# Attention's softmax sums applied at the output projection's loads, and the last input chunks in another order

## The chip, the cores and the metric

The kernel runs on one core of a Trainium2 chip. The metric is the device time of the whole kernel in microseconds (us); lower is better. Five engines work side by side, each strictly in the order of its own instructions: TensorE (PE, matrix products and transposes), VectorE (DVE), ScalarE (ACT, activations and copies), GpSimd (POOL) and SyncE (SP), which here only issues DMA transfers. An instruction that waits holds up everything behind it on its engine.

## The reference

One encoder layer over a 1024 x 1024 activation: an input projection feeds two head groups side by side, 8 attention heads (64 wide, 2 key/value heads) and 4 heads of a bidirectional mLSTM; an output projection and a SwiGLU feed-forward follow. What the change touches is the softmax of the attention and the projection that reads it:

```python
def one_block(q_blk):
    s = jnp.einsum('bkgqd,bksd->bkgqs', q_blk, kt).astype(jnp.float32) * scale
    p = jax.nn.softmax(s, axis=-1).astype(vt.dtype)
    return jnp.einsum('bkgqs,bksd->bkgqd', p, vt)
...
    mix = jnp.concatenate([y_attn, y_mem], axis=-1) @ w_out[l]
    x = x + g1[:, None, :] * mix
```

Softmax divides each row of exponentials by its sum. The division is by a number of that query row alone, so it may be done on the probabilities or, later, on the attention's output.

## The kernel before

Nearly every product is made of three matmuls on a high and a low part of each operand (`mm3`, lines 322 to 325), so every operand tile is split: ACT copies it into the high part, then DVE or POOL subtracts that from the original to get the low part.

The program is written out by a planner. `Clock` (line 131) keeps estimated times of the engines and a heap of steps; `ck.chain(delay, steps...)` runs steps one after another when their flags are set; `ck.streams(mains, fills)` writes PE's work: whichever main stream is ready goes first, and a fill stream goes when none is. The estimates only set the order in which instructions stand; on the chip each engine follows that order and waits on semaphores. Where this text says that something "stands" somewhere, it speaks of that order.

The stages: the head of the kernel (adaLN, the first projections, up to about 150 us of the profile), attention (about 153 to 484 us), mLSTM with the output projection (to about 680 us), the feed-forward (the rest).

**Attention.** There are 64 steps q, 8 heads times 8 blocks of 128 query rows (`NQ`, `NJ`). `scores` computes a 128 x 1024 score tile in PSUM (`S`), DVE takes its row maximum (`top`), ACT makes the exponentials into the tile `P` with their row sum (`exp`), DVE takes the reciprocal of the sum, POOL multiplies the whole tile `P` by it (`norm`). Only then is the flag `Pok[q]` set, on which `turned` waits: it transposes `P` on PE in two halves into PSUM tiles `T`, ACT and DVE split them into `PT`. `values` multiplies `PT` with the values into `av`, and each pair of steps stores 64 x 256 outputs, `avt`, to the DRAM tile `ya_d`. `colq` (line 308) is a 128 x 8 x 8 tile that holds the scale factor of each query row and head, read as the scale of `exp` and in `top`. `att_q(h)` loads and splits the queries of head h into `qs`.

**Fills in attention.** The rest of the input projection runs in the gaps, in the order of the list `IN` (line 49): "q" units are queries, "f" units (`conv_unit`) make 512-column products, copied out of PSUM as `xp` and then run through a five-tap convolution on DVE (`y`), "t" units (`chunk_unit`) make eight 256-column chunks each, copied out as `vstg` and stored to `v_d` or `o_d`. In attention the fills have one PSUM bank ("acc" and "acct" with one buffer between them): a next unit can start only when ACT has copied the last one out. Besides, `ada_late` streams 64 tiles of the adaLN weights through POOL (a multiplication, `ada`) and ACT (their sum).

**The output projection.** `load_y` (line 1274) loads four 128 x 512 tiles `yat` for each half of the columns and each of the two head groups (`ya_d` for attention, `ym_d` for mLSTM) and splits them into `yah` on ACT and `yal` on POOL. The first call of it, for attention's first half, is made while the last chunk unit ("t", 3) runs beside the start of mLSTM. `mq` are the query tiles of mLSTM, loaded one ahead, `wv` its weighted values on POOL. All loads and stores named here are issued by SP, through the helper `dma`.

Of the kernel before, what the change touches and what calls it, by code (L numbers as in the profile page):

```python
# [11 lines left out]
F32 = mybir.dt.float32  # L12
F32R = mybir.dt.float32r
BF16 = mybir.dt.bfloat16
AF = mybir.ActivationFunctionType
OP = mybir.AluOpType
# [4 lines left out]
P = 128  # L21
S = 1024
D = 1024
KT = D // P
HALF = 512
NH = 2
NJ = S // P
EPS = 1e-6
QK = 0.25 * 128 ** -0.5
AH = 8  # L30
DH = 64
# [15 lines left out]
AHEAD = 2  # L47
NP = NF // 2
IN = [("q", 2), ("q", 3), ("f", 0), ("f", 4), ("t", 2), ("f", 1),
      ("f", 5), ("f", 2), ("t", 1), ("f", 6), ("f", 3), ("f", 7), ("t", 3)]  # L50
MIX = [("o", i) for i in range(16)] + [("m", (i + 8) % 16) for i in range(16)]
FF = [("b", p) for p in range(NB)] + [("v", 0)] + [("s", (p, i)) for p in range(1, NP - 1) for i in range(2)] + [("v", NP - 1)]
SET = ["A11", "A12", "S2", "S3", "S1", "A22", "S4"]
# [207 lines left out]
def layer_kernel(ctx, tc, xT, c, w_ada, vecs, cons, rope, w_f, w_fT, w_t0, w_t, w_o, w_gu, w_d, out):  # L261
# [39 lines left out]
    mqk_d = [dram.tile([P, S], F32, name=f"mqk_d{i}") for i in range(8)]  # L301
    v_d = [dram.tile([P, NJ, 2, P], F32, name=f"v_d{i}") for i in range(2)]
    o_d = [dram.tile([P, NJ, 2, P], F32, name=f"o_d{i}") for i in range(2)]
    ya_d = [dram.tile([P, S], F32, name=f"ya_d{i}") for i in range(4)]
    x1_d = [dram.tile([P, S], F32, name=f"x1_d{i}") for i in range(KT)]
    act_d = [{m: dram.tile([P, HALF], F32, name=f"act_d{p}{m}") for m in DOWN} for p in range(NP)]
# [25 lines left out]
    def halves(n):  # L332
        return slice(n * HALF, (n + 1) * HALF)
# [42 lines left out]
    with tc.manual_schedule():  # L376
# [801 lines left out]
        def att_q(h):  # L1178
            if h:
                qd = ap.tile([P, S], F32, tag="qd", name="qd", bufs=1)  # L1180
                src = q_d[h // 2][(h % 2) * DH:(h % 2 + 1) * DH]
                dma(qd[0:DH], src)
                there = ck.chain(dma(qd[DH:P], src), lambda: None)
            else:
                qd, there = q0_at
            qs = ap.tile([P, S], F32R, tag="qs", name="qs")
            Q[h] = qs, ck.chain(0.0, there, lambda: act.activation(qs, qd, AF.Copy),
                                lambda: (gps if h else dve).tensor_sub(qs[DH:P], qd[DH:P], qs[DH:P].bitcast(F32)))

        def scores():  # L1190

            for q in range(NQ):
# [18 lines left out]

                def exp(st=st, sp=sp, cq=cq, q=q, f=f):
                    Pt[q] = ap.tile([P, S], F32, tag="P", name="P", bufs=3)
                    act.activation(Pt[q], sp, AF.Exp, bias=st[:, 1:2], scale=cq, accum_out=st[:, 2:3])
                    f.set(ck, ck.fin + LAT)

                def norm(st=st, q=q):
                    gps.tensor_scalar(Pt[q], Pt[q], st[:, 3:4], 0.0, op0=OP.mult, op1=OP.add)

                ck.chain(LAT, top, exp, lambda st=st: dve.reciprocal(st[:, 3:4], st[:, 2:3]), norm, flag=Pok[q])  # L1220

        def turned():

# [50 lines left out]
        def load_y(mem, n):  # L1274
# [6 lines left out]
            for k in range(4):  # L1281
                if mem and k == MH - 1:
                    Y[mem, n].append(y_last[n])
                    continue
                e = [None, None, Flag()]
                Y[mem, n].append(e)

                def load(e=e, k=k):
                    t = op.tile([P, HALF], F32, tag="yat", name="yat", bufs=4)
                    arrive = dma(t, (ym_d if mem else ya_d)[k][:, halves(n)])  # L1290

                    def hi():
                        e[0] = op.tile([P, HALF], F32R, tag="yah", name="yah", bufs=yb)
                        act.activation(e[0], t, AF.Copy)

                    def lo():
                        e[1] = op.tile([P, HALF], F32R, tag="yal", name="yal", bufs=yb)
                        gps.tensor_sub(e[1], t, e[0].bitcast(F32))

                    ck.chain(arrive, *used, hi, lo, flag=e[2])  # L1300

                ck.chain((2.0 if mem else 0.0) + (2.5 * k if at else 0.0), *([ym_ok[k][n]] if mem else []), load)

# [1089 lines left out]
```

## Time and profile before

| what | us |
|---|---|
| median of 3 runs (lowest, highest) | 1325.05 (1324.91, 1332.57) |
| the profiled execution's own time | 1328.24 |
| its span, first to last instruction | 1326.4 |
| PE busy (share of the span) | 1268.8 (96%) |
| DVE busy | 1044.1 (79%) |
| ACT busy | 705.8 (53%) |
| POOL busy | 524.5 (40%) |

The page of the profile lists each engine's busy time, the span in 40 slices, the chain of work that ended last, and groups of instructions. Group lines read: source line, engine, operation, output<-input, shape, count | busy us, mean ns of one | idle time just before them, and what ended most of it. L102 is the line of the helper that records all DVE, ACT and POOL operations, so there the tile's name tells them apart. In a timeline the first two columns are the start and the duration in us, and brackets give the idle time before an instruction and who ended it. PEclk is the share of its full clock that PE was granted.

### The profile page before, as it was taken

How to read it: one execution, taken by the hardware profiler on the slowest of the kernel's cores; microseconds unless marked ns; L12 is line 12 of the kernel's file. 1: busy time of each engine (PE TensorE's matmuls, PEld its weight loads, DVE VectorE, ACT ScalarE, POOL GpSimd, SP SyncE). 2: the span in 40 equal slices, each digit the busy share in tenths (PEclk: the TensorE clock that was granted, in tenths of full speed). 3: DMA queues.
4: the chain of work that ended last, by engine and by line, in shares of the span. 5: the costliest groups of instructions: out<-in, count | busy, mean ns of one | idle time of the engine just before them, and what ended most of it. 6: DMA issues, size and time to landing. Idle time of an engine off the chain costs nothing.

```text
span 1326.4 us, 19735 instructions
## 1 busy us (share of the span) xinstructions
PE 1268.8 (96%) x6656; PEld 1071.9 (81%) x6656; DVE 1044.1 (79%) x1679; ACT 705.8 (53%) x1349; POOL 524.5 (40%) x455
## 2 busy tenths in 40 slices
PE   9999789999899999999999999999999998999997
PEld 7887678878887888787877888888888886888886
DVE  7958798879578956898789988866676755788886
ACT  6583667877587746555686332233332334454453
POOL 0072467766476515532153355544555420000002
PEclk9999899999999999999999999999999999999999
DMA  9547423333233237633552443323333259733324
GB/s 375 196 151 196 127 99 121 96 94 106 81 120 94 64 117 259 202 100 124 191 184 71 159 135 128 112 104 115 109 104 110 88 192 335 274 100 93 94 60 163
DMA packets 104469, 187.04 MB, mean 141 GB/s; under 512 B 11568, under 2 KB 33200, under 8 KB 104368
## 3 DMA queue, kind: packets, MB, share of 16 engines
q1 hardware_dynamic: 91120, 163.81, 38.1%
q10 hardware_dynamic: 13248, 21.97, 4.4%
q8 instruction: 53, 0.87, 0.3%
q14 instruction: 48, 0.39, 0.1%
HBM read 139.33 MB, written 42.73 MB: 137 GB/s over the span
## 4 chain that ended last, share of the span: by engine, by line
PE 65%; DVE 16%; ACT 6%; DMA 5%; issue 4%; POOL 4%; SPq 0%; ACTq 0%; DVEq 0%; POOLq 0%
PE acc L325 16%; PE acc L323 16%; PE acc L324 16%; DVE x L102 3%; PE av L1255 3%; PE T L1234 3%; PE S L1202 2%; DVE sst L102 2%; DVE y L102 2%; DVE PT L102 2%; DVE wlo L102 1%; PE acct L323 1%; POOL wlo L102 1%; PE acct L325 1%; PE acct L324 1%
## 5 line engine op out<-in xcount | busy, mean ns | idle before, releaser
L102 ACT ACTIVATE whi<-wst 128x512 fp32r<-128x512 f32 (+2 forms) x223 | 133.9, 607 | 140.8 <-PE acc L325 62.7
L102 POOL TENSOR_TENSOR wlo<-wst,whi 128x512 fp32r<-128x512 f32 x80 | 123.2, 1547 | 162.3 <-ACT whi L102 110.9
L324 PE MATMUL acc<-x,whi 128*128 128x512 f32 x352 | 136.9, 389 | 0.0
L102 DVE TENSOR_TENSOR wlo<-wst,whi 128x512 fp32r<-128x512 f32 (+2 forms) x143 | 94.3, 664 | 33.2 <-ACT whi L102 32.8
L102 POOL TENSOR_SCALAR P<-P,sst 128x1024 f32<-128x1024 f32 x64 | 84.3, 1319 | 77.3 <-DVE sst L102 69.0
L102 DVE TENSOR_TENSOR PT<-T,PT 128x512 fp32r<-128x512 f32 x128 | 84.8, 682 | 24.7 <-ACT PT L102 24.4
L323 PE MATMUL acc<-hh,whi 128*128 128x512 f32 x224 | 96.2, 429 | 8.4 <-ACT xp L102 8.4
L102 POOL TENSOR_TENSOR x<-x,ny 128x256 f32<-128x256 f32 (+1 forms) x8 | 8.3, 1066 | 237.3 <-PE acc L325 217.1
L102 POOL TENSOR_TENSOR wlo<-wr,whi 128x512 fp32r<-128x512 f32 x52 | 72.2, 1388 | 71.8 <-ACT whi L102 68.7
L325 PE MATMUL acc<-whi,wcl 128*128 128x512 f32 x244 | 96.6, 396 | 2.6 <-DVE wcl L102 2.6
L323 PE MATMUL acc<-whi,wch 128*128 128x512 f32 x244 | 96.2, 394 | 2.3 <-ACT wch L102 2.3
L324 PE MATMUL acc<-wlo,wch 128*128 128x512 f32 x244 | 95.9, 393 | 0.0
L324 PE MATMUL acc<-hl,whi 128*128 128x512 f32 x224 | 88.7, 396 | 0.3 <-DVE hl L102 0.3
L102 ACT ACTIVATE whi<-wr 128x512 fp32r<-128x512 f32 x56 | 35.4, 632 | 100.6 <-DVE wr L102 48.3
L102 POOL TENSOR_TENSOR ada<-ada,cond 128x512 f32<-128x512 f32 x55 | 78.6, 1435 | 25.7 <-DMA ada<-in_w_ada_dram 22.6
L325 PE MATMUL acc<-hh,wlo 128*128 128x512 f32 x224 | 88.7, 396 | 0.1
L102 ACT ACTIVATE P<-S,sst,colq 128x1024 f32<-128x1024 f32 x64 | 77.2, 1206 | 21.1 <-DVE sst L102 20.7
L102 ACT ACTIVATE PT<-T 128x512 fp32r<-128x512 f32 x128 | 73.5, 597 | 26.7 <-PE T L1234 25.4
L323 PE MATMUL acct<-whi,hh 128*128 128x256 f32 (+1 forms) x256 | 77.6, 303 | 9.5 <-ACT vstg L102 8.8
L102 DVE TENSOR_REDUCE sst<-S 128x1 f32<-128x1024 f32 x64 | 77.7, 1214 | 6.2 <-PE S L1202 5.1
L1234 PE MATMUL T<-ident,P 128*128 128x128 f32 x512 | 72.8, 274 | 6.6 <-DVE PT L102 4.0
L324 PEld LDWEIGHTS acc<-x,whi 128*128 128x128 f32 x352 | 66.1, 188 | 13.7
(483 smaller groups left out, 3836.6 us busy)
## 6 DMA issues: line engine op xcount, KB each, us to landing
wr<-in_w_gu_dram SPq DMA_DIRECT2D x66, 256.0 KB, 2.7
ada<-in_w_ada_dram SPq DMA_DIRECT2D x64, 256.0 KB, 2.9
wd<-in_w_d_dram SPq DMA_DIRECT2D x22, 512.0 KB, 6.9
wst<-in_w_gu_dram SPq DMA_DIRECT2D x42, 256.0 KB, 2.9
wst<-act_d SPq DMA_DIRECT2D x33, 256.0 KB, 3.1
ada<-in_w_ada_dram SPq DMA_DIRECT2D x16, 512.0 KB, 7.4
wst<-in_w_o_dram SPq DMA_DIRECT2D x32, 256.0 KB, 3.3
act_d<-sg ACTq DMA_DIRECT2D x29, 256.0 KB, 2.1
```

The lines of the kernel that those rows point to most:

```text
L102: return fn(*args, **kw)
L323: nc.tensor.matmul(acc, w[0], x[0], start=first, stop=False)
L324: nc.tensor.matmul(acc, w[0], x[1], start=False, stop=False)
L325: nc.tensor.matmul(acc, w[1], x[0], start=False, stop=last)
L1202: nc.tensor.matmul(sp[:, halves(n)], qs[:, j * P:(j + 1) * P], k2[g][m][:, halves(n)], start=m == 0, stop=m == 1)
L1234: nc.tensor.transpose(tp[:, k], Pt[q][:, (4 * b + k) * P:(4 * b + k + 1) * P], ident)
L1255: nc.tensor.matmul(av, va[:, k, h // 4], PT[it, b][m][:, k - 4 * b], start=(k, m) == (0, 0), stop=(k, m) == (NJ - 1, 1))
```

## The change

The division by the softmax sums moves. `norm` and the reciprocal of each step are gone, and `Pok[q]` is set when `exp` is done. `exp` now writes its sum into the element of `colq` that it has just used as its scale. After the last block of a head one reciprocal is taken of the head's 128 x 8 column of `colq`, and SP stores it, element by element, to a DRAM row of 1024 numbers, `r_d[h]`. When `load_y` loads a tile of attention's output it also loads, into a tile `yar` of which there are two, the two rows of reciprocals that belong to it, each one spread over 64 partitions, and POOL multiplies `yat` by `yar` before the split. Besides, `att_q(0)` waits for the flag `logf_ok` of the gate computation in the planner, and in `IN` the unit ("t", 1) stands after ("f", 6) and ("f", 3).

```diff
-      ("f", 5), ("f", 2), ("t", 1), ("f", 6), ("f", 3), ("f", 7), ("t", 3)]
+      ("f", 5), ("f", 2), ("f", 6), ("f", 3), ("t", 1), ("f", 7), ("t", 3)]
...
+    r_d = [dram.tile([1, S], F32, name=f"r_d{i}") for i in range(AH)]
...
-            Q[h] = qs, ck.chain(0.0, there, lambda: act.activation(qs, qd, AF.Copy),
+            Q[h] = qs, ck.chain(0.0, there, *([] if h else [logf_ok]), lambda: act.activation(qs, qd, AF.Copy),
...
-                    act.activation(Pt[q], sp, AF.Exp, bias=st[:, 1:2], scale=cq, accum_out=st[:, 2:3])
+                    act.activation(Pt[q], sp, AF.Exp, bias=st[:, 1:2], scale=cq, accum_out=cq)
                     f.set(ck, ck.fin + LAT)
-                def norm(st=st, q=q):
-                    gps.tensor_scalar(Pt[q], Pt[q], st[:, 3:4], 0.0, op0=OP.mult, op1=OP.add)
-
-                ck.chain(LAT, top, exp, lambda st=st: dve.reciprocal(st[:, 3:4], st[:, 2:3]), norm, flag=Pok[q])
+                ck.chain(LAT, top, exp, flag=Pok[q])
+                if j == NJ - 1:
+                    rq = colq[:, :, h]
+                    ck.chain(1.0, *Pok[q - j:q + 1], lambda rq=rq: dve.reciprocal(rq, rq),
+                             lambda rq=rq, h=h: dma(r_d[h].rearrange("o (j p) -> p (o j)", p=P), rq), bg=[None] * NJ + ["dve", None])
...
                     t = op.tile([P, HALF], F32, tag="yat", name="yat", bufs=4)
+                    r = None if mem else op.tile([P, HALF], F32, tag="yar", name="yar", bufs=2)
+                    for i in range(0 if mem else 2):
+                        dma(r[i * DH:(i + 1) * DH], r_d[2 * k + i][:, halves(n)].partition_broadcast(DH))
                     arrive = dma(t, (ym_d if mem else ya_d)[k][:, halves(n)])
...
-                    ck.chain(arrive, *used, hi, lo, flag=e[2])
+                    ck.chain(arrive, *used, *([] if mem else [lambda: gps.tensor_mul(t, t, r)]), hi, lo, flag=e[2])
```

The planner makes a new order of all engines from this. Three places of it follow. A name in brackets after a row is an engine or a DMA queue that it waits for; the number behind such a name has no meaning here.

The first place is ACT at the start of attention. `Fr<-T` is a step of the gate computation that reads what `logf` leaves, `qs<-qd` is the split of the first queries, `xp<-acc` empties the PSUM bank of a fill. Before:

```order
L102 ACTIVATE xp<-acc 128x512 [waits PE_49]
L102 ACTIVATE qs<-qd_1337 128x1024 [waits DMAHW0_49,DVE_49,Pool_49]
L102 ACTIVATE xp<-acc 128x512 [waits PE_49]
L102 ACTIVATE Fr<-T_1373 64x1024
L102 ACTIVATE whi<-wst 128x512 [waits DMAHW7_49,PE_49]
```

After:

```order
L102 ACTIVATE xp<-acc 128x512 [waits PE_49]
L102 ACTIVATE Fr<-T_1381 64x1024 [waits DVE_49]
L102 ACTIVATE qs<-qd_1345 128x1024 [waits DMAHW0_49,Pool_49]
L102 ACTIVATE xp<-acc 128x512 [waits PE_49]
L102 ACTIVATE whi<-wst 128x512 [waits DMAHW7_49,PE_49]
```

The 64 x 1024 copy `Fr` has moved ahead of `qs` and ahead of the second `xp`.

The second place is POOL in attention's second head. Before:

```order
L102 TENSOR_SCALAR P<-P,sst 128x1024 x2
L102 TENSOR_TENSOR ada<-ada,cond 128x512 x2
L102 TENSOR_SCALAR P<-P,sst 128x1024 x2
L102 TENSOR_TENSOR ada<-ada,cond 128x512 x2
L102 TENSOR_SCALAR P<-P,sst 128x1024
L102 TENSOR_TENSOR qs<-qd,qs 64x1024
L102 TENSOR_SCALAR P<-P,sst 128x1024
```

After:

```order
L102 TENSOR_TENSOR ada<-ada,cond 128x512
L102 TENSOR_TENSOR wlo<-wst,whi 128x512
L102 TENSOR_TENSOR qs<-qd,qs 64x1024
L102 TENSOR_TENSOR wlo<-wst,whi 128x512
L102 TENSOR_TENSOR ada<-ada,cond 128x512 x6
```

The 64 rows on `P` are gone from POOL; what is left are the adaLN products and the low parts. On DVE the 64 reciprocals of `sst` are gone and 8 of `colq` have come. PE has the same instructions as before.

The third place is SP where the output projection's first tiles are loaded, at the start of mLSTM. `yar<-r_d` are the reciprocals, `mq` is the second query tile of mLSTM. Before:

```order
L328 DMA yat<-ya_d_101 128x512
L328 DMA yat<-ya_d_102 128x512
L328 DMA yat<-ya_d_103 128x512 [waits DMAHW0_49]
L328 DMA yat<-ya_d_104 128x512 [waits DMAHW1_49]
L328 DMA o_d_100<-vstg 128x256 [waits DMAHW2_49,Activation_49]
L328 DMA mq<-mqk_d_89 128x256 [waits DMAHW3_49]
```

After (one `yar` pair and `yat` stand ahead of the first row):

```order
L329 DMA yar<-r_d_103 64x512 [waits DMAHW1_49]
L329 DMA yar<-r_d_104 64x512 [waits DMAHW2_49]
L329 DMA yat<-ya_d_110 128x512 [waits DMAHW3_49]
L329 DMA yar<-r_d_105 64x512 [waits DMAHW6_49,DMAHW7_49,DMAHW4_49,Pool_49]
L329 DMA yar<-r_d_106 64x512 [waits DMAHW5_49]
L329 DMA yat<-ya_d_111 128x512
L329 DMA yar<-r_d_107 64x512 [waits DMAHW2_49,DMAHW1_49,Pool_49]
L329 DMA yar<-r_d_108 64x512 [waits DMAHW0_49]
L329 DMA yat<-ya_d_112 128x512
L329 DMA o_d_100<-vstg 128x256 [waits Activation_49]
L329 DMA mq<-mqk_d_89 128x256 [waits DMAHW3_49]
```

Eight loads of `yar` have come in, and two of them wait for POOL, since there are only two tiles `yar`; the load of `mq` stands behind them.

## The prediction

> **What bounds the kernel now.** I read the page first: the span, the busy times, and the chain of work that ended last.
>
> ```profile
> span 1326.4 us, 19735 instructions
> PE 1268.8 (96%) x6656; PEld 1071.9 (81%) x6656; DVE 1044.1 (79%) x1679; ACT 705.8 (53%) x1349; POOL 524.5 (40%) x455
> PE 65%; DVE 16%; ACT 6%; DMA 5%; issue 4%; POOL 4%; SPq 0%; ACTq 0%; DVEq 0%; POOLq 0%
> ```
>
> PE is busy for 1268.8 of 1326.4 us, and the change takes no instruction from it. So a gain can only come out of the 57.6 us in which PE stands idle, and only out of the part that lies where the change works. That is attention, so the next view is the busy time by stretches, and then who PE, and ACT behind it, waited for between 153 and 490 us.
>
> ```profile
> 153.60:483.90 330.30, 306.93 (x2028) 271.74 (x2026) 271.86 (x428) 241.34 (x483) 208.96 (x161) 1.00 0.31 94
> ...
> PE acct L323 <- ACT vstg L102: 8.8, 9, 2.0
> PE T L1234 <- DVE PT L102: 4.0, 6, 1.6
> PE acc L323 <- ACT xp L102: 3.6, 2, 2.9
> PE S L1202 <- ACT P L102: 3.2, 1, 3.2
> PE T L1234 <- POOL P L102: 2.0, 3, 1.6
> PE av L1255 <- DVE PT L102: 1.4, 3, 0.7
> PE acct L323 <- ACT xp L102: 0.7, 1, 0.7
> ...
> ACT ada L102 <- POOL ada L102: 19.6, 13, 3.9
> ```
>
> The stretch's row gives its length, then PE, PEld, DVE, ACT and POOL busy, the clock, and DMA. In 330.3 us PE is idle for 23.4; the waits listed sum to 23.7, in 25 stalls of at most 3.2 us. That is the whole prize in attention. Only 2.0 us of it stand under POOL's name; the largest entries name ACT's copies out of the fills' one PSUM bank. But ACT itself stood 19.6 us waiting for POOL's adaLN products, and POOL works in order, with the 64 normalisations between those products.
>
> **The change part by part.**
>
> *Normalisation and reciprocals leave.* What they hold is in the group lines of the page and of the lines view.
>
> ```profile
> L102 POOL TENSOR_SCALAR P<-P,sst 128x1024 f32<-128x1024 f32 x64 | 84.3, 1319 | 77.3 <-DVE sst L102 69.0
> L102 DVE RECIPROCAL sst<-sst 128x1 f32<-128x1 f32 x64 | 10.0, 157 | 16.6 <-ACT P L102 16.2
> ```
>
> POOL loses 64 x 1.319 = 84.3 us of its 209 in attention, DVE 64 x 0.157 = 10.0 of its 272 and gets 8 small reciprocals back (8 x 0.157 = 1.3, an estimate from the same row). None of these is on PE, so they count only through stalls. I followed the longest of those back. The one at 427 us, in the timelines of PE, ACT and POOL:
>
> ```profile
> 427.45 0.50 PE L323 MATMUL acc<-hh,whi 128*128 128x512 f32 x1 [2.91 <-ACT xp L102]
> 426.19 0.63 ACT L102 ACTIVATE ada<-ada 128x512 f32<-128x512 f32 x1 [2.12 <-POOL ada L102]
> 426.82 0.58 ACT L102 ACTIVATE xp<-acc 128x512 f32<-128x512 f32 x1
> 421.94 2.02 POOL L102 TENSOR_SCALAR P<-P,sst 128x1024 f32<-128x1024 f32 x1 [1.89 <-DVE sst L102]
> 423.92 2.23 POOL L102 TENSOR_TENSOR ada<-ada,cond 128x512 f32<-128x512 f32 x1
> ```
>
> Read from below: a normalisation of 2.02 us, the adaLN product behind it, ACT's sum waiting 2.12 us for that, the copy `xp` behind the sum, and PE 2.91 us idle. Without the normalisation the product can start at once and the chain is gone. Two more stalls have the same shape:
>
> ```profile
> 174.21 0.39 PE L323 MATMUL acct<-whi,hh 128*128 128x256 f32 x1 [2.00 <-ACT vstg L102]
> 168.85 2.09 POOL L102 TENSOR_SCALAR P<-P,sst 128x1024 f32<-128x1024 f32 x1
> 170.90 2.22 POOL L102 TENSOR_TENSOR ada<-ada,cond 128x512 f32<-128x512 f32 x1
> ...
> 336.87 0.38 PE L323 MATMUL acct<-whi,hh 128*128 128x256 f32 x1 [1.63 <-ACT vstg L102]
> 331.95 2.09 POOL L102 TENSOR_SCALAR P<-P,sst 128x1024 f32<-128x1024 f32 x1
> 334.01 1.29 POOL L102 TENSOR_TENSOR ada<-ada,cond 128x512 f32<-128x512 f32 x1
> ```
>
> These three and the 2.0 us under POOL's own name make 2.91 + 2.00 + 1.63 + 2.0 = 8.5 us that I can tie to the normalisations. The 3.2 us of `S <- ACT P` belong to attention's start, costed apart. Of the remaining 23.7 - 8.5 - 3.2 = 12.0 us I take a quarter, 3, as relieved too: transposes may start one normalisation sooner and DVE is less full, but several of these stalls hang on gate steps or on ACT's own queue, and the new order will bring stalls of that kind of its own. Term: -11.5 us; bounds 0 (every stall is replaced) and -23.7 (all gone). What is late next is ACT's copies out of the one fill bank.
>
> *Attention's start (`att_q(0)` behind `logf`).* The head's last stall and its cause:
>
> ```profile
> 147.72 0.79 PE L323 MATMUL acc<-hh,whi 128*128 128x512 f32 x1 [4.81 <-ACT xp L102]
> 146.13 1.06 ACT L102 ACTIVATE qs<-qd 128x1024 fp32r<-128x1024 f32 x1 [3.70 <-issue]
> 147.69 1.06 ACT L102 ACTIVATE Fr<-T 64x1024 f32<-64x1024 f32 x1
> 143.88 2.17 DVE L102 SCALAR_TENSOR_TENSOR T<-T,gt 64x1024 f32<-64x1024 f32 x1
> 132.00:165.00 33.00, 25.02 (x110) 20.06 (x110) 25.24 (x33) 21.10 (x30) 15.54 (x12) 0.90 0.43 132
> ```
>
> `qs` starts when the `logf` step on DVE ends (143.88 + 2.17 = 146.05), and PE waits for the `xp` behind `qs`. The new order doesn't mend that: `Fr`, which reads the same result, now stands first, so `xp` comes 1.06 us later and the 4.81 become about 5.9. Against that more fill stands between the first scores and the first transposes, which can take up a part of the 3.2 us that PE lost there. Term: +1; bounds -3.2 (that stall gone) and +3 (both worse by their 1.06, and one more).
>
> *The stores of the reciprocals.* Eight stores of 1024 single numbers. No row shows a transfer in so small pieces. The nearest rows by the number of pieces, and by the bytes:
>
> ```profile
> v<-v_d SPq DMA_DIRECT2D x4, 512.0 KB, 6.5
> ya_d<-avt SPq DMA_DIRECT2D x32, 64.0 KB, 1.9
> ```
>
> `v` is 128 x 8 runs, so also 1024 pieces: 6.5 us to landing; `avt`, 64 KB, takes 1.9. Nobody reads the rows before attention is over, so only what queues behind them could feel it: 0 if hidden, 8 x (6.5 - 1.9) = 37 if each delay came through to PE. I take 0, since SP stands waiting most of the time and the loads behind are for later steps.
>
> *The new loads and products of the output projection.* Sixteen loads of `yar` (128 KB each) and eight products on POOL (1.435 us each by the row of `ada`, an operation of the same shape, so 11.5 in all). They lie beside PE's work except at the first call, where SP is the matter. Timelines of SP and PE and the DMA rows there:
>
> ```profile
> 495.04 2.20 SPq L328 DMA_DIRECT2D yat<-ya_d  x4
> 498.62 0.32 SPq L328 DMA_DIRECT2D mq<-mqk_d  x1
> 505.30 0.61 PE L2015 MATMUL tr<-mq,mk 128*128 128x128 f32 x4
> 510.21 0.40 PE L323 MATMUL acc<-yah,whi 128*128 128x512 f32 x1
> 483.90:531.00 47.10, 44.66 (x299) 39.92 (x300) 24.31 (x70) 23.14 (x69) 21.27 (x50) 1.00 0.73 239
> ...
> yat<-ya_d SPq DMA_DIRECT2D x8, 256.0 KB, 5.9
> mq<-mqk_d SPq DMA_DIRECT2D x16, 128.0 KB, 3.1
> L102 POOL TENSOR_TENSOR ada<-ada,cond 128x512 f32<-128x512 f32 x55 | 78.6, 1435 | 25.7 <-DMA ada<-in_w_ada_dram 22.6
> ```
>
> With the first call at the same place: two `yar` and the first `yat` are issued by about 496; the tile lands 5.9 us later, near 502; the product ends near 503.4; only then may SP issue the third `yar`. The fourth waits for the second product, near 504.8. Three issues of about 0.45 and the store later, `mq` goes out near 506.5 instead of 498.62 and lands 3.1 us later, near 509.6. PE wants it at 505.30, in front of all its work, so it stands about 4.3 us. The split tiles for 510.21 are then late by less than that shift: the last product needs a `yat` issued near 505.7, so near 511.6, and its low part follows near 516, where PE, 4.3 late, wants it near 518. Term: +4; bounds 0 (PE reaches that point late anyway) and +8 (the loads land as much later as the extra megabyte delays them, and PE's clock falls).
>
> On the clock: the 4.81 us stall above lowered PE's granted clock to 0.90 of the stretch from 132 to 165 us, so 3.3 us of full clock; all of attention, with the 2.91 us stall in it, has a clock of 1.00 in the first row on stretches. A stall of 4.3 is between. The Trainium skill, page "TensorE: Matmul & The Clock Gate", section "HAM oscillation — how this bites in real kernels", gives as its rule of thumb no idle gaps over about 3.4 us; by that rule this stall would cost some 3 us more, and the sum would be 1321 rather than 1318. The two stalls of this trace agree with it. I leave it out of the sum, as the 4.3 hangs on a chain of landings, and have it in the bound.
>
> *Order of the last chunks.* Three fills change places; the same fills lie in attention before and after, and ("t", 3) is still the last. I take 0: the cover is that PE has fill work left up to attention's end; if that ran out, one chunk's copy out of PSUM would show, as in the rows of `vstg`, at up to 2.0 us each.
>
> **The sum.** -11.5 + 1 + 0 + 4 + 0 = -6.5. Against the profiled execution's own 1328.24 (its span of 1326.4 and 1.8 around it) that is 1321.7. That execution lay 3.2 above the median of the runs shown, 1325.05; against the median the sum gives 1318.5, and I say 1318.
>
> **The rivals.** *All of attention's stalls go.* For it: DVE, ACT and POOL would be at 80%, 73% and 38% of attention's time, and the loop from exponentials to transposes is shorter. Against it: one PSUM bank for the fills, and stalls that come of ACT's order. It gives 1325 - 23.7 + 1 + 4, about 1306.
>
> *The relief is hidden.* PE is the bound, the stalls are those of a fixed order, and the new order has as many. For it: only 2.0 us are under POOL's name. Then the time is 1325 + 1 + 4, about 1330, and the change does nothing that shows.
>
> *SP becomes the bound at mLSTM's start (slower).* One mechanism: SP, held by the third `yar` until a product on POOL is done, holds back `mq`, and PE stands in front. For it: the DMA engines are busy for 0.73 of that stretch already, against 0.31 in attention, and in the new order POOL has other work (`wv`) between those products, so the wait may be longer than I reckon. Against it: it happens once with nothing to cover it; the second call spreads its loads. `mq` has 3.6 us of slack (landed near 501.7, wanted at 505.3), so the delay of 8 us that I reckon costs 4.3. It decides from a delay of some 14 us on, which costs PE the 10.5 that the change gains elsewhere. With a delay of 30 us it costs 26: about 1325 - 10.5 + 26 = 1340.
>
> **How the numbers follow.** The forecast gets 0.55 (1310 to 1325), all stalls gone 0.20, hidden 0.15, SP 0.10. The range 1303 to 1329 leaves out SP, half of the 0.15 (above 1329) and a little at the low end, 0.2 in all. All terms at their ends on one side would give 1298 or, without the stores, 1336 (with them 1373); I trim these, since the ends hardly fall together. A measurement of this kernel can tell about 1% from no change, 13 us: faster than 1312 are the second case and a small part of the forecast's, together 0.27; slower than 1338 is the SP case but for its mild end, 0.09; within 1% the rest, 0.64.
>
> **What would show it.** In the profile after: POOL in attention near 125 us instead of 209; no `P` rows on POOL; ACT's wait for `ada` well under 19.6 us; PE's idle time in attention near 13 instead of 23.4. At attention's start a PE stall of 5 to 6 us before `acc`. At mLSTM's start a row of PE waiting for `mq` by about 4 us, and SP waiting for POOL. I am wrong if attention's idle time stays above 20 us, if `mq` is in time, or if PE waits anywhere for a load that stands behind a store of reciprocals.

## The result and the profile after

| | median, us | lowest to highest | ratio to the kernel before, 95% interval |
|---|---|---|---|
| before, measured beside it | 1326.28 | 1324.91 to 1332.57 | |
| after | 1395.94 | 1391.11 to 1397.01 | 1.0503 (1.0480 to 1.0527) |

The change makes the kernel 5% slower, some 70 us where 6.5 fewer were forecast. The profiled execution took 1391.11 us, with a mean granted clock of 0.971 of TensorE's full speed; before it was 0.991. The page of the changed kernel, its span, busy times, DMA packets, and the chain that ended last:

```profile
span 1389.2 us, 19520 instructions
PE 1284.1 (92%) x6656; PEld 1087.0 (78%) x6656; DVE 1039.6 (75%) x1623; ACT 705.5 (51%) x1349; POOL 447.9 (32%) x399
DMA packets 114068, 189.16 MB, mean 136 GB/s; under 512 B 20144, under 2 KB 41776, under 8 KB 113968
PE 59%; DVE 17%; DMA 11%; ACT 5%; issue 4%; POOL 3%; SPq 1%; ACTq 0%; DVEq 0%; POOLq 0%
```

PE, DVE and ACT have no more to do than before (PE's 15 us more are the same matmuls at the lower clock), and POOL has 76.6 us less. What grew is DMA in the chain, from 5% to 11%, and the packets under 512 B, from 11,568 to 20,144. So the place to look is where an engine waits for a load. In the changed kernel attention lasts from 155.8 us (first scores) to 538.8 (last product with V); the stretches of that part, with PE, PEld, DVE, ACT and POOL busy, the clock, the DMA share and GB/s:

```profile
155.80:538.80 383.00, 320.48 (x2015) 284.13 (x2014) 263.52 (x370) 240.04 (x482) 123.56 (x97) 0.92 0.31 81
198.00:231.00 33.00, 24.73 (x173) 23.11 (x172) 20.84 (x27) 18.31 (x38) 10.05 (x7) 0.90 0.32 91
330.00:363.00 33.00, 21.82 (x112) 18.08 (x111) 17.45 (x25) 14.79 (x30) 11.70 (x10) 0.79 0.31 89
396.00:429.00 33.00, 22.73 (x142) 20.54 (x141) 17.04 (x24) 15.93 (x33) 12.51 (x8) 0.84 0.40 96
```

PE stands idle for 383.0 - 320.5 = 62.5 us of attention, where it was 23.4, and the clock of the whole part is 0.92 instead of 1.00. Next, who was waited for between 155 and 539 us (total us, times, longest):

```profile
ACT ada L102 <- POOL ada L102: 29.6, 7, 10.1
...
PE T L1236 <- DVE PT L102: 22.2, 9, 10.3
...
ACT qs L102 <- DMA qd<-q_d: 22.0, 4, 10.8
...
PE acc L324 <- ACT xp L102: 17.3, 4, 10.8
...
PE av L1257 <- ACT PT L102: 13.0, 2, 8.3
...
ACT whi L102 <- DMA wst<-in_w_f_dram: 10.2, 1, 10.2
```

Before, no wait of PE in attention was over 3.2 us; now they reach 10.8. All three names behind PE's waits are copies that ACT makes or feeds, and ACT waits for loads: for queries (`qd`) and for weights (`wst`). One of these stalls in full, in the timelines of SP, ACT and PE; the stores of the reciprocals are the rows `r_d<-colq`:

```profile
192.17 0.39 SPq L329 DMA_DIRECT2D r_d<-colq  x1
...
194.38 1.11 SPq L329 DMA_DIRECT2D qd<-q_d  x2
...
207.65 1.06 ACT L102 ACTIVATE qs<-qd 128x1024 fp32r<-128x1024 f32 x1 [8.60 <-DMA qd<-q_d]
...
210.50 1.12 PE L1236 MATMUL T<-ident,P 128*128 128x128 f32 x4 [7.49 <-DVE PT L102]
```

The store takes SP 0.39 us. The queries issued 2.2 us behind it land some 12 us later, ACT's split of them waits 8.60 us, everything queued behind it on ACT (the copies of transposed probabilities among it) waits too, and PE stands for 7.49 us. What the DMA engines did meanwhile, in steps of 3 us:

```profile
192.00:195.00 3.00, 3.00 (x24) 2.82 (x23) 2.94 (x5) 2.95 (x8) 0.00 (x0) 1.00 0.51 123
195.00:198.00 3.00, 3.00 (x28) 3.00 (x27) 2.45 (x4) 1.78 (x6) 1.29 (x1) 1.00 0.30 2
198.00:201.00 3.00, 3.00 (x24) 2.83 (x23) 2.06 (x3) 1.05 (x3) 0.00 (x0) 1.00 0.21 31
201.00:204.00 3.00, 2.02 (x14) 1.64 (x12) 0.07 (x1) 0.00 (x0) 0.00 (x0) 1.00 0.42 31
204.00:207.00 3.00, 0.00 (x0) 0.00 (x0) 0.00 (x0) 0.00 (x0) 0.00 (x0) 1.00 0.70 212
```

From 195 to 198 us, with queries, results and adaLN weights issued, the DMA engines move 2 GB/s, then 31 GB/s until 204, and they are recorded as busy for only 0.21 to 0.42 of these 9 us; only then 212 GB/s. By the last row PE, DVE, ACT and POOL all stand. The DMA rows (count, KB each, median us from issue to landing) of the changed kernel:

```profile
qd<-q_d SPq DMA_DIRECT2D x16, 256.0 KB, 10.4
...
r_d<-colq SPq DMA_DIRECT2D x8, 4.0 KB, 12.4
```

A store of 4 KB takes 12.4 us to land, and the loads of queries have gone from 4.1 to 10.4. Theory: the 1024 single numbers of a store occupy what all transfers share, and loads issued behind it come late. Rivals: it is SP's queue alone (another queue would mend it); it is the new order of the engines and not the stores; the stores cost little and the removed normalisations or the new loads did harm.

### The profile page after: what moved, and what is told of

It is laid out like the page before. It is cut to its first block, busy times and chain, and to the rows that moved or that the text cites. A ratio compares the mean times of both kernels' runs of the same rounds, so it can differ in the third digit from the quotient of the medians.

```text
span 1389.2 us, 19520 instructions
## 1 busy us (share of the span) xinstructions
PE 1284.1 (92%) x6656; PEld 1087.0 (78%) x6656; DVE 1039.6 (75%) x1623; ACT 705.5 (51%) x1349; POOL 447.9 (32%) x399
## 2 busy tenths in 40 slices
DMA packets 114068, 189.16 MB, mean 136 GB/s; under 512 B 20144, under 2 KB 41776, under 8 KB 113968
## 4 chain that ended last, share of the span: by engine, by line
PE 59%; DVE 17%; DMA 11%; ACT 5%; issue 4%; POOL 3%; SPq 1%; ACTq 0%; DVEq 0%; POOLq 0%
PE acc L324 16%; PE acc L326 16%; PE acc L325 16%; DMA ada<-in_w_ada_dram 3%; DMA qd<-q_d 3%; DVE x L102 3%; PE T L1236 2%; DVE y L102 2%; DVE sst L102 2%; PE av L1257 2%; PE S L1203 2%; DVE PT L102 1%; POOL wlo L102 1%; DVE hs L102 1%; POOL hl L102 1%
## 5 line engine op out<-in xcount | busy, mean ns | idle before, releaser
L1257 PE MATMUL av<-PT,va 128*128 128x256 f32 x512 | 75.8, 294 | 14.2 <-ACT PT L102 13.0
L1236 PEld LDWEIGHTS T<-ident,P 128*128 128x128 f32 x512 | 61.1, 145 | 32.6 <-DVE PT L102 26.4
L102 DVE TENSOR_REDUCE sst<-S 128x1 f32<-128x1024 f32 x64 | 77.8, 1215 | 11.5 <-PE S L1203 11.3
L1257 PEld LDWEIGHTS av<-PT,va 128*128 128x128 f32 x512 | 69.9, 198 | 18.5 <-ACT PT L102 14.1
```

Of the source, the lines that this page charges most:

```text
L102: return fn(*args, **kw)
L1236: nc.tensor.transpose(tp[:, k], Pt[q][:, (4 * b + k) * P:(4 * b + k + 1) * P], ident)
L1257: nc.tensor.matmul(av, va[:, k, h // 4], PT[it, b][m][:, k - 4 * b], start=(k, m) == (0, 0), stop=(k, m) == (NJ - 1, 1))
```

## The experiments

Ratios are to the kernel before, measured beside each; an interval is of 95%. Where two variants are compared, their ratios are subtracted, 0.1% being 1.33 us.

**Stores in longer runs.** The changed kernel, with the same order of every engine but the pieces of each store: partition after partition, 128 runs of 32 B.

```diff
-                    ck.chain(1.0, *Pok[q - j:q + 1], lambda rq=rq: dve.reciprocal(rq, rq),
-                             lambda rq=rq, h=h: dma(r_d[h].rearrange("o (j p) -> p (o j)", p=P), rq), ...
+                    rc = ap.tile([P, NJ], F32, tag="rc", name="rc", bufs=2)
+                    ck.chain(1.0, *Pok[q - j:q + 1], lambda rq=rq, rc=rc: dve.reciprocal(rc, rq),
+                             lambda rc=rc, h=h: dma(r_d[h].rearrange("o (p j) -> p (o j)", j=NJ), rc), ...
```

> The changed kernel with its eight stores of reciprocals made of 128 runs of 32 bytes instead of 1024 single numbers of 4 bytes; the same 4 KB each, and the same order of every engine. The numbers land in the rows in another order, so the attention part of the output is scaled by the wrong reciprocals. Theory A (the pieces: a store of 1024 single numbers holds up the loads issued behind it by some 10 us, and ACT and PE stand): about 1318 us, between 1305 and 1335, no PE stall over 4 us in attention after its start. Theory B (the new order of the instructions is bad in itself): stays near 1395, with the same eight stalls.

Measured: 1325.23 us, ratio 0.9962 (0.9947 to 0.9977). Attention's stretch, and who waited in it:

```profile
157.10:474.40 317.30, 303.96 (x2015) 270.30 (x2014) 261.68 (x368) 239.65 (x482) 127.11 (x97) 1.00 0.32 97
```

```profile
PE T L1237 <- DVE PT L102: 4.1, 7, 0.8
...
ACT ada L102 <- POOL ada L102: 10.1, 5, 4.2
```

The same work with PE idle for 317.3 - 304.0 = 13.3 us and a clock of 1.00: the whole loss is gone, 5.03% and 0.38%, together some 72 us. So neither the order nor the removed and added work did it: the pieces of the store did (their number and their size change together here). Packets under 512 B are 12,976 here and 20,144 in the changed kernel; the difference, 7168, is 8 x (1024 - 128), so each single number went as a packet of its own. The Trainium skill, page "DMA: Bandwidth & Descriptors", section "Rules for kernel authors", says that a strided last dimension lowers to one descriptor for each element; this count agrees.

Of the 65.7 us by which attention is longer with the small pieces (383.0 against 317.3), 62.5 - 13.3 = 49.2 are idle time of PE and 320.5 - 304.0 = 16.5 are the same matmuls at a lower clock.

**Another queue.** The changed kernel, with the stores issued on ACT's DMA queue.

```diff
-   dma(r_d[h].rearrange("o (j p) -> p (o j)", p=P), rq)
+   dma(r_d[h].rearrange("o (j p) -> p (o j)", p=P), rq, nc.scalar)
```

> The changed kernel with the eight stores of single numbers issued by ACT, on ACT's own DMA queue, instead of SP. Theory A1 (the pieces hold the 16 DMA engines or the way to memory, for every queue): 1380 to 1400, the loads land as late as before. Theory A2 (only what queues behind on SP's own queue waits): about 1320, loads of SP land in their usual 3 to 4 us while the store takes its 10. Theory B (order): 1390 or more.

Measured: 1373.47 us, ratio 1.0323 (1.0284 to 1.0362). The first stall again, in the timelines of ACT and SP:

```profile
193.90 0.39 ACTq L329 DMA_DIRECT2D r_d<-colq  x1
...
195.26 1.29 SPq L329 DMA_DIRECT2D qd<-q_d  x2
...
208.22 1.06 ACT L102 ACTIVATE qs<-qd 128x1024 fp32r<-128x1024 f32 x1 [7.95 <-DMA qd<-q_d]
```

The queries no longer stand behind a store in SP's queue and still land late. Neither theory's time came (1380 to 1400, or about 1320): against the 32-byte runs this loses 3.6%, 48 us, where the store on SP loses 72. So the queue is about a third of it; two thirds go through what the queues share. The Trainium skill, same page, section "Issuing engines are not separate DMA queues", says that transfers from any engine end up on the same 16 DMA engines; the 48 us agree with it.

**The stores alone.** The kernel before, plus eight stores of 1024 single numbers (of `colq`, into rows that nobody reads).

```diff
+                if j == NJ - 1:
+                    rq = colq[:, :, h]
+                    ck.chain(1.0, *Pok[q - j:q + 1],
+                             lambda rq=rq, h=h: dma(r_d[h].rearrange("o (j p) -> p (o j)", p=P), rq))
```

> The kernel before with nothing but eight stores of single numbers added, one after each head, from the tile of scale factors; nobody reads them. Theory A: 1326 plus most of the loss, 1370 to 1400, a PE stall of 4 to 11 us after each store. Theory B: 1326 to 1332, since the order hardly moves.

Measured: 1357.57 us, ratio 1.0200 (1.0181 to 1.0219), so 27 us. The DMA row, and PE's longest entries in attention:

```profile
r_d<-colq SPq DMA_DIRECT2D x8, 4.0 KB, 10.6
```

```profile
PE T L1239 <- DVE PT L102: 15.3, 10, 6.7
PE av L1260 <- ACT PT L102: 6.3, 2, 4.1
```

The stores alone cost the kernel before 2%, less than the 1370 to 1400 us of theory A and more than the 1326 to 1332 of B. But the same eight cost 72 us in the new order. In the changed kernel a load of queries or of the fills' weights is issued within 3 us behind five of the eight; here behind three. Whether that is the reason is the next experiment.

**The stores six issues later.** The changed kernel; PE, ACT, DVE and POOL have the same order row for row, and SP issues each store behind the next six transfers.

```diff
+    tardy = []
-    def dma(dst, src, q=None):
-        (q or nc.sync).dma_start(dst, src)
+    def dma(dst, src, q=None, hold=0):
+        if hold:
+            tardy.append([hold, dst, src])
+        else:
+            (q or nc.sync).dma_start(dst, src)
+            for e in tardy:
+                e[0] -= 1
+            while tardy and tardy[0][0] == 0:
+                nc.sync.dma_start(*tardy.pop(0)[1:])
...
-   dma(r_d[h].rearrange("o (j p) -> p (o j)", p=P), rq)
+   dma(r_d[h].rearrange("o (j p) -> p (o j)", p=P), rq, hold=6)
```

> The changed kernel with each store of reciprocals issued six issues later on SP, behind the load of the next queries (or of weights) that stood right behind it; the order of PE, ACT, DVE and POOL is the same row for row. Theory that the eight stores cost about 70 us instead of the 27 that they cost in the order of before because of what is issued right behind each: ACT's waits for qd of 8 to 11 us go from most heads, and the time falls from 1396 to about 1350 to 1365. Rival, that a store of single numbers takes its 10 us from whatever comes, and fills follow everywhere: the waits move to wst and ada, and the time stays between 1380 and 1400.

Measured: 1360.91 us, ratio 1.0236 (1.0218 to 1.0254). SP and ACT at the first store, and the DMA row of the queries:

```profile
196.01 1.29 SPq L334 DMA_DIRECT2D qd<-q_d  x2
...
200.30 0.43 SPq L338 DMA_DIRECT2D r_d<-colq  x1
...
201.14 1.06 ACT L102 ACTIVATE qs<-qd 128x1024 fp32r<-128x1024 f32 x1
```

```profile
qd<-q_d SPq DMA_DIRECT2D x16, 256.0 KB, 4.1
```

The queries are in time here (no idle time ahead of `qs`, landing 4.1 us as before; over all heads ACT waits for queries once, 3.5 us, where it was four times, 22.0), and 2.7%, 36 us, of the 72 are gone, within the range of the first theory. The other half stays: later loads take the delay (ACT waits 10.0 us in all for `wst` of the fills in three places, PE 7.8 us for mLSTM's first keys behind the last store). So the place of such a store decides half of its price.

**Consecutive addresses.** The changed kernel; still 1024 single numbers, but their places in DRAM lie side by side instead of 512 B apart.

```diff
-   dma(r_d[h].rearrange("o (j p) -> p (o j)", p=P), rq)
+   dma(r_d[h].rearrange("o (p j) -> p (o j)", j=NJ), rq)
```

> The changed kernel with one edit: each store still moves 1024 single numbers, since its source lies strided in SBUF, but their places in DRAM are consecutive (partition after partition) instead of 512 B apart. The rows then hold the reciprocals in another order, so attention's output is scaled by the wrong ones. Theory that the number of 4-byte pieces sets the price: nothing changes, r_d lands after 9.5 us or more, the time stays near 1396, and certainly above 1380. Rival that the scattered addresses set it (each piece in a 512 B block of its own): r_d lands in 2 to 5 us and the time falls to about 1325 to 1335, as with 128 runs of 32 B. In between (1340 to 1380) both count.

Measured: 1368.46 us, ratio 1.0294 (1.0262 to 1.0325). The DMA rows:

```profile
qd<-q_d SPq DMA_DIRECT2D x16, 256.0 KB, 8.6
...
r_d<-colq SPq DMA_DIRECT2D x8, 4.0 KB, 8.6
```

Neither theory alone: the store lands in 8.6 us instead of 12.4, and the loss is 3.3%, 44 us. The scattering of the addresses makes about 28 of the 72 us, the single pieces the rest. Whether it is their number or their 4 bytes these runs do not tell apart: the load of `v`, also 1024 pieces but of 512 B, lands in 6.5 us.

**Reciprocals turned before the store.** For each head the 128 x 8 reciprocals are transposed on PE and stored as 8 runs of 512 B.

```diff
+                    def turn(rc=rc, tr=tr):
+                        tr.append(psum_tile([P, 4, P], "T"))
+                        nc.tensor.transpose(tr[0][0][0:NJ, 0], rc, ident)
...
+                    def rows8(tr=tr):
+                        tr.append(ap.tile([DH, 2, P], F32, tag="avt", name="avt", bufs=3)[0:NJ, 0])
+                        dve.tensor_copy(tr[1], tr[0][0][0:NJ, 0])
...
+                    ck.chain(1.0, ..., lambda: dve.reciprocal(rc, rq), (slot("T"), turn), rows8,
+                             lambda tr=tr, h=h: dma(r_d[h].rearrange("o (j p) -> (o j) p", p=P), tr[1]), ...
```

> The changed kernel with each head's 128 x 8 reciprocals transposed on PE (one small transpose, one DVE copy), so that the store has 8 runs of 512 bytes; the output is the reference's. Theory A: 1305 to 1335, at or a little below the kernel before, with the 4.4 us stall for mq at mLSTM's start still there. Theory B: near 1395.

Measured: 1335.83 us, ratio 1.0038 (1.0021 to 1.0054). The time is just above the 1305 to 1335 of theory A. The stores no longer cost what they did, but 0.76%, 10 us, against the 32-byte runs are lost again. In its profile attention is 4.0 us longer (321.3 against 317.3), and PE's longest wait for mLSTM's queries is 6.0 us instead of 4.2; the rest was not traced.

**One store for all heads.** One reciprocal of the 64 columns after the last exponentials, one transpose, one copy, one store of 64 runs of 512 B. The second variant has four buffers for `yar` instead of two.

```diff
-                if j == NJ - 1:
+                if q == NQ - 1:
...
+                        dve.reciprocal(tr[0].rearrange("p h j -> p j h"), colq)
...
+                        nc.tensor.transpose(tr[1][0][0:AH * NJ, 0], tr[0].rearrange("p h j -> p (h j)"), ident)
...
+                             lambda: dma(r_d.rearrange("h (j p) -> (h j) p", p=P), tr[2]))
...
-   r = None if mem else op.tile([P, HALF], F32, tag="yar", name="yar", bufs=2)
+   r = None if mem else op.tile([P, HALF], F32, tag="yar", name="yar", bufs=4)
```

> The changed kernel, but the sums of all eight heads are inverted at once after the last exponentials (one reciprocal of 128x64 on DVE), turned by one transpose on PE and one copy on DVE, and stored as 64 runs of 512 B. Seven of eight transposes, small copies and stores of the variant with turned reciprocals are gone. Theory that the small pieces were all that went wrong, and that the turning per head cost that variant its 10 us against the one with 32-byte runs: attention comes to 316 to 319 us from its first scores to its last product, the sum to about 1320 to 1326, ratio 0.994 to 0.999. Rival, that late reciprocals cost more: the loads of yar stand behind the store, so the first split tile of the output projection comes late by its landing of about 2 us or more, and the time is near 1330 or above.

> The variant with one store of all reciprocals, with four buffers of yar instead of two, so that SP does not wait for POOL's products before it issues mq. Theory of the prediction for the stall at mLSTM's start (mq held on SP by the third yar): PE's wait for mq falls from about 4.2 us to under 1.5, and the time by 2 to 4 us against the variant with two buffers. Rival: mq or the split tiles are late anyway because the loads share the DMA engines, the wait stays above 3 us or moves to the split tiles, and the time does not change by more than 1.5.

Measured: two buffers 1327.26 us, ratio 0.9985 (0.9972 to 0.9999); four buffers 1323.64, ratio 0.9958 (0.9943 to 0.9974). With two buffers the time is 0.53%, 7 us, better than with the turning for each head, and just above the 1320 to 1326 that the theory gave. Attention lasts 302.1 us, not 316 to 319, since a part of the fills now stands behind it (1949 matmuls of PE in it instead of 2015). PE's wait for mLSTM's queries with two buffers, and with four:

```profile
500.89 1.20 PE L2036 MATMUL tr<-mq,mk 128*128 128x128 f32 x4 [4.61 <-DMA mq<-mqk_d]
```

```profile
496.67 0.68 PE L2036 MATMUL tr<-mq,mk 128*128 128x128 f32 x4 [1.93 <-DMA mq<-mqk_d]
```

The wait shrinks by 2.7 us and the time by 0.27%, 3.6 us, as the theory of SP held by POOL's products says, though 1.9 us stay where under 1.5 were expected. The shorter stall also spares the clock. The stretch of 33 us from some 11 us ahead of the stall, with two buffers and with four:

```profile
490.00:523.00 33.00, 27.15 (x159) 23.55 (x157) 19.34 (x50) 17.42 (x49) 21.06 (x32) 0.90 0.79 245
```

```profile
485.00:518.00 33.00, 28.86 (x183) 24.65 (x181) 21.33 (x52) 17.73 (x50) 22.66 (x37) 1.00 0.93 274
```

**The two edits on the order.** On top of the one store, the chunks' order and the wait of the first queries on `logf` undone, together with two buffers, then alone and together with four.

```diff
-IN = [..., ("f", 5), ("f", 2), ("f", 6), ("f", 3), ("t", 1), ("f", 7), ("t", 3)]
+IN = [..., ("f", 5), ("f", 2), ("t", 1), ("f", 6), ("f", 3), ("f", 7), ("t", 3)]
...
-            Q[h] = qs, ck.chain(0.0, there, *([] if h else [logf_ok]), lambda: ...
+            Q[h] = qs, ck.chain(0.0, there, lambda: ...
```

> The variant with one store of all reciprocals, with the two edits on the order undone: the last chunks as before, and the first head's queries not behind the logf step. It tells what these two edits are worth. Theory of the prediction (start +1, order of the chunks 0): within 2 us of the variant with the new order. Rival, that the new order was needed to keep fill work for PE up to attention's end: 3 to 8 us slower. Rival, that the later start costs what it shows (first scores 2 to 3.5 us later): 2 to 3 us faster.

> The variant with one store of all reciprocals and four buffers of yar, and with the first head's queries not behind the logf step; the last chunks in the new order. With both edits on the order undone the variant with two buffers was 4.6 us slower. If the chunks' order is what was worth that, this one is as fast as with the wait, or 1 to 3 us faster since the first scores come earlier (1320 to 1324 where the other was 1323.6). If the wait on logf is what was worth it, this one is 3 to 6 us slower (1327 to 1330).

> The variant with one store and four buffers of yar, with only the last chunks put back in the old order (the first head's queries still behind logf). With it and the next one, the two edits on the order stand alone and together, all with one store and four buffers. If the edits add up (logf worth 12 us, as its removal cost, and the new chunks worth -7, worked out from the variant with both undone), this one is the fastest of the four, 1315 to 1319. If each schedule has its own stalls and nothing adds up, it lies between 1322 and 1335.

> The variant with one store and four buffers of yar, with both edits on the order undone. If the four buffers are worth the 3.6 us here that they were worth in the new order, it comes to about 1328 (1326.5 to 1329.5), within 0.3% of the kernel before: then the removal of the normalisations alone is worth little more than the new loads cost. Rival, that the relief of POOL is worth the 11.5 us of the prediction in any order: 1322 or below.

Measured, with two buffers and both undone: 1331.82 us, ratio 1.0020 (1.0006 to 1.0034), 0.35% or 4.7 us behind the new order: the size that the first rival gave, but, as the others show, not for its reason. With four buffers:

| | new order of the chunks | old order of the chunks |
|---|---|---|
| first queries behind `logf` | 1323.64 us, 0.9958 (0.9943 to 0.9974) | 1321.92 us, 0.9948 (0.9929 to 0.9966) |
| not behind it | 1335.36 us, 1.0047 (1.0029 to 1.0064) | 1329.04 us, 0.9996 (0.9980 to 1.0012) |

The wait on `logf` is worth 0.5% (old chunks) to 0.9% (new ones), 6 to 12 us. The new order of the chunks is worth nothing with it and costs 0.5% without it, so the two don't add up, and the wait, not the chunks, is what the new order gains by. Both forecasts that took the two for sums missed (1335.36 is worse than either case of its expectation); that for both undone with four buffers, about 1328, came out (1329.04). What the wait does is seen at attention's start. PE's two stalls there and the stretch from 140 to 170 us, first with both edits undone:

```profile
148.87 0.80 PE L324 MATMUL acc<-hh,whi 128*128 128x512 f32 x1 [5.68 <-ACT xp L102]
...
161.92 1.97 PE L1252 MATMUL T<-ident,P 128*128 128x128 f32 x8 [2.68 <-ACT P L102]
```

```profile
140.00:170.00 30.00, 21.60 (x93) 17.58 (x92) 26.19 (x33) 17.09 (x28) 14.20 (x10) 0.83 0.29 93
```

and with the new order:

```profile
148.35 0.80 PE L324 MATMUL acc<-hh,whi 128*128 128x512 f32 x1 [5.50 <-ACT xp L102]
...
158.84 0.39 PE L324 MATMUL acct<-whi,hh 128*128 128x256 f32 x1 [1.42 <-ACT xp L102]
```

```profile
140.00:170.00 30.00, 22.18 (x121) 18.62 (x120) 29.51 (x36) 17.82 (x33) 15.89 (x12) 0.89 0.38 126
```

The first stall is about the same. The second is 1.3 us shorter, since fills stand between the first scores and the first transposes, and the clock is 0.89 instead of 0.83. With both edits undone it falls a second time, to half, right behind the stall of 2.68 us:

```profile
161.90:164.90 3.00, 2.98 (x11) 2.76 (x12) 1.92 (x1) 3.00 (x6) 2.33 (x3) 0.50 0.06 23
```

That is about 3 us here (1.3 and 0.06 x 30). The second fall doesn't come every time: with two buffers and both undone the same stall is 3.38 us long and the clock of the 30 us is 0.89. With the new chunks the whole difference lies between the first scores and the first product with `mq`, 341.8 us without the wait and 329.3 with it: 7.1 of these 12.5 us are idle time of PE, 5.4 the same work at a lower clock. Which waits make them, beyond this first one, was not told apart.

With the four-buffer variants, two versions beat the kernel before and the changed one: 0.9958 and 0.9948. Their intervals overlap, so which is the better is open.

## Why the prediction failed

**The stores, taken at 0: this step failed.** "Nobody reads the rows before attention is over, so only what queues behind them could feel it" named the right victim. "I take 0, since SP stands waiting most of the time and the loads behind are for later steps" was no reason in either half. SP's time was never the matter: the issue takes 0.39 us, and moving the store to another queue leaves 48 of the 72 us. And that a load is for a later step doesn't make it harmless: the queries split at 207.65 us are for scores that PE begins at about 232, but ACT's order has their split ahead of copies that PE needs at once. The order of SP after the change could have shown the danger: at six of the eight stores the loads of `qd` stand directly behind `r_d` or up to four issues after it. The bound, 37 us, was too small as well, for two reasons that the runs show. The row of `v`, 1024 runs of 512 B in 6.5 us, stood in for 1024 single numbers, which take 12.4 (8.6 if their places are consecutive; the same bytes in 128 runs of 32 B take 1.5). And a delay was priced at its own length, while a stall of 5 to 11 us also lowers the clock: 16.5 us of attention's loss is that.

**Normalisation and reciprocals, -11.5: the sum came out with the new order, the relief alone is smaller.** With 32-byte runs attention's idle time is 13.3 us, as forecast ("near 13"), ACT's wait for `ada` is 10.1 instead of 19.6, POOL is busy for 127.1 ("near 125"), and attention is 328.6 - 317.3 = 11.3 us shorter (it lasted from 153.56 to 482.19 before). But that has the new order in it. With both edits on the order undone, one store and four buffers, PE's waits up to mLSTM's start (first product with `mq`) are these, in total us, times and longest, and ACT's wait for `ada`:

```profile
PE T L1252 <- DVE PT L102: 6.6, 9, 1.9
...
PE T L1252 <- ACT P L102: 2.7, 1, 2.7
...
ACT ada L102 <- POOL ada L102: 7.8, 5, 3.9
```

All of PE's waits there sum to 16.3 us; before they sum to 25.0 over the same work, and the stretch from the first scores to the first product with `mq` takes 335.9 us instead of 343.7. So the relief alone is about 8 us. The time of that variant, ratio 0.9996 (0.9980 to 1.0012), shows that nearly all of it is taken back elsewhere. In its profile 1.6 us go ahead of attention (first scores at 155.2 instead of 153.6) and 6.9 in the stage that has the new loads and products, from the first product with `mq` to ACT's first split of the feed-forward's weights `wr`. This stage before, in this variant, and in the changed kernel:

```profile
497.30:729.80 232.50, 224.97 (x1132) 185.07 (x1133) 197.89 (x417) 143.38 (x313) 89.39 (x118) 0.99 0.49 161
491.10:730.50 239.40, 225.93 (x1134) 185.38 (x1135) 203.89 (x417) 143.39 (x314) 101.92 (x125) 1.00 0.53 166
553.60:795.10 241.50, 226.34 (x1131) 187.19 (x1132) 201.40 (x417) 143.09 (x311) 98.30 (x125) 0.99 0.51 164
```

PE's idle time in it grows from 7.5 us to 13.5 and 15.2. In this variant PE waits there 3.0 us for `num`, a tile that DVE makes in mLSTM, instead of 0.6, 2.5 for `mq` instead of 1.0, and 1.6 for `yal`, which it did not wait for before. Why `num` comes late was not traced.

**Attention's start, +1: wrong in sign.** The head's stall came as worked out, 5.92 us after the change against "about 5.9". But "more fill stands between the first scores and the first transposes, which can take up a part of the 3.2 us" was given too little weight: the edit gains 6 to 12 us, beyond the bound of -3.2, which looked at the one stall and not at the clock nor at the schedule behind it.

**New loads and products, +4: right at the stall, too small for the stage.** PE waited 4.44 us for `mq` in the changed kernel, against "about 4.3"; four buffers take 2.7 us off such a stall. But the whole stage is 241.5 - 232.5 = 9.0 us longer (rows above), more than the bound of +8, since "They lie beside PE's work except at the first call" did not hold. The rows of the stall in the changed kernel:

```profile
565.31 0.43 SPq L329 DMA_DIRECT2D mq<-mqk_d  x1
...
568.62 0.68 PE L2020 MATMUL tr<-mq,mk 128*128 128x128 f32 x4 [4.44 <-DMA mq<-mqk_d]
```

**Order of the last chunks, 0: right** where the first queries wait for `logf`, as they do in the change: 0.9958 against 0.9948, overlapping.

**The sum without the stores**, -6.5, is what the 32-byte runs show: -0.38% (-0.53 to -0.23), -5.1 us (-7.0 to -3.1). It held although three terms were off: the start gained, which made up for the smaller relief and the dearer stage of the new loads. There is luck in it too. In the profiled executions the variant with 32-byte runs begins the feed-forward only 0.9 us ahead of the kernel before (first split of `wr` at 728.9 against 729.8); the other 3.7 us of its lead arise in the feed-forward, where both do the same work and which takes 592.6 to 596.9 us over the fourteen profiles of this text.

**The rivals.** None of the three took place; the slower one looked for SP at mLSTM's start, and the loss lay in attention. Without the single-number stores and the edits on the order the outcome is that of the second rival, nothing that shows (0.9996), but not by its way: the relief came, and the later stage took it back. The sentence on what would prove the prediction wrong, "if PE waits anywhere for a load that stands behind a store of reciprocals", names what happened.

**The clock.** The sum left out that a stall of 4.3 us lowers the clock. With 4.61 us the clock was 0.90 in the 33 us around it, with 1.93 it was 1.00 (both above), with the 4.44 of the changed kernel 0.95, and in the 33 us around attention's stalls of 7 to 11 us it was 0.79 to 0.90. The rule cited there, no idle gaps over about 3.4 us (the Trainium skill, page "TensorE: Matmul & The Clock Gate", section "HAM oscillation — how this bites in real kernels"), agrees with these. As a safe bound it does not hold here: the clock fell to half after the 2.68 us at attention's start with both edits undone (above), while it stayed at 1.00 after stalls of 2.91 and 3.18 us in the kernel before. What decides between them no run here shows.

## What to carry to other kernels

Look at a transfer's pieces before its bytes: here a side output of 4 KB, laid across partitions, went out one number at a time and delayed loads that were issued behind it while it took its 9 to 12 us, on another queue too. Turn it into rows first, or store it in runs that the layout gives for nothing (the loads must then undo the other order, which no run here tried), and look in the queue's order at what stands right behind it and which engine waits for that. And when a removed cost and a new order come in one change, price them apart: here the sum of the other terms came out right with three of them wrong.

## What the runs showed that was not expected

- 1024 single numbers, 4 KB in all, took 12.4 us to land with their places 512 B apart and 8.6 us with consecutive places; 4 KB in 128 runs of 32 B took 1.5 us, and 32 KB in 64 runs of 512 B 2.5 us. While one of the first kind was under way, all DMA engines together moved 2 GB/s for 3 us.
- Eight such stores cost 27 us in the kernel before and 36, 48 or 72 in the changed one, by what stands behind them and on which queue. Why single pieces slow the other transfers so, inside the DMA engines or at the memory, no run here tells apart.
